# A two-layer decoder trunk on one core: a planner that simulates the timeline in place of the default planner

## The chip, the cores and the metric

The kernel runs on one core of a Trainium2 chip, as one launch. A core has five engines that each work through a queue of their own: TensorE (PE in the profile, with its weight loads shown apart as PEld), VectorE (DVE), ScalarE (ACT), GpSimd (POOL) and SyncE (SP), which here only issues DMA transfers. They wait for each other by semaphores. The metric is the device time of the launch in microseconds; lower is better.

## The reference

The input is one sequence of 512 tokens with 1024 features, in float32. Layer 0 runs multi-head latent attention (MLA, 8 heads) and differential attention (4 heads, each with two score matrices) side by side behind one input projection, layer 1 dilated attention (three groups of 4 heads) and stick-breaking attention (4 heads). Each mixer is followed by a gated ConvFFN of width 2816, and both are wrapped in RMSNorms with a residual.

```python
for i in range(DEPTH):                      # DEPTH = 2
    h = rms_norm(x, pre_g)
    h = even_mixer(h, ...) if i % 2 == 0 else odd_mixer(h, ...)
    x = x + rms_norm(h, post_g)
    h = conv_ffn(rms_norm(x, ffn_pre_g[i]), ffn_w_up[i], ffn_conv_w[i], ffn_conv_b[i], ffn_w_down[i])
    x = x + rms_norm(h, ffn_post_g[i])

# the differential heads of even_mixer, for one block of 128 queries
def probs(qb, kf):
    s = jnp.einsum('bhqd,bhkd->bhqk', qb, kf).astype(jnp.float32) * scale + bias   # ALiBi
    return jax.nn.softmax(jnp.where(causal, s, -jnp.inf), axis=-1)
p = probs(a1, k1) - lam * probs(a2, k2)
o = jnp.einsum('bhqk,bhkd->bhqd', p.astype(v.dtype), v)
o_diff = rms_norm(o_diff, subln_g) * (1.0 - lam_init)

# the stick-breaking heads of odd_mixer
log_beta = jax.nn.log_sigmoid(z)
log_keep = jnp.where(strict, jax.nn.log_sigmoid(-z), 0.0)
after = lax.cumsum(log_keep, axis=3, reverse=True) - log_keep
a = jnp.where(strict, jnp.exp(log_beta + after), 0.0)

def conv_ffn(h, w_up, conv_w, conv_b, w_down):
    gate, up = jnp.split(causal_dwconv(h @ w_up, conv_w, conv_b), 2, axis=-1)
    return (jax.nn.silu(gate) * up) @ w_down
```

## The kernel before

**Products.** Every float32 product with a weight is done as three products of a shorter type. An operand is split into a high part, cast on ACT, and a remainder, subtracted on DVE; `mm3` (L263 to L265) then issues high × high, high × low and low × high into one PSUM bank. Weights come in units of 128 x 1024: SP loads the raw unit, ACT casts it (`wh`, L72) and DVE subtracts (`wl`, L73). The class `Weights` holds several units loaded ahead and splits them ahead of their use. Activations are split by the helper `split` (L171, L172).

**Stages.** The program runs `even`, `ffn(0)`, `odd`, `ffn(1)` one after the other. The 512 tokens are four tiles of 128 rows; the results of the projections are held by feature or by token as the next stage needs them. PSUM banks are handed out under five tags: `a` (3 banks), `s` (2), `t`, `o` and `n` (1 each). A new use of a bank waits for the last reader of the old one.

**The attention stages.** `skewed` (L270 and following) runs a list of units in a software pipeline that is written out by hand: in one step it issues the scores of unit n, the transposes of unit n−1, the value product of unit n−2 and so on, and after every so many steps it takes one of a list of *fillers*, pieces of projection work that are independent of the units.

- In the even mixer, MLA comes first: 32 units of head and query tile (`score` with the reduction L593 and the exponential L597, `turn`, `value` L750). Its fillers are the four `diff_v` pieces (`av`, value projection of the differential heads, L755 to L769), which in program order stand at the end.
- Then come the differential heads: 16 units, four query tiles for each of four heads. `score` issues two score products (L827, one bank each) under `tc.high_priority()`, two reductions with the ALiBi table (L593), two exponentials (L597), and the combination of the two (L838 to L841). `turn` transposes it (L604) and copies it out of PSUM (L607 on ACT, L609 on DVE), `value` multiplies by the values (L852), scales (L854) and squares for the mean (L856 on ACT); POOL computes the reciprocal root (`rr`, L178 and L181) and `norm` applies it (L863). `finish` transposes a head's four tiles (`tpo`, L870) and splits them (`odh`, `odl`).
- The fillers of the differential heads, one every second step, are six groups of query and key projections (`aqk`, `diff_qk`, L622 to L631, 24 matmuls each) and four pieces of the output projection (`ao`, `project`, L880 to L895), whose MLA half needs only the MLA results `omh`, `oml`.
- The tables of the differential heads come by DMA from ACT's queue: `subg` (L780), `lamb` (L782) and `alibi` (L786). `lamb` leads to the scalar `neglam` (L790 to L796). They lie in a pool whose space comes free with the MLA stage.
- In the odd mixer the stick-breaking heads go through `sb_scores` (L1025 and following, Exp at L1044), `sb_softplus` (Ln at L1049) and `sb_weights` (split `sh`, `sl`, then the suffix sums as products `cp`, L1064, and Exp at L1068). Exp and Ln need different tables of ACT, and a change of table is an ACT_TABLE_LOAD of 1.28 us. The dilated heads follow as two pipelines with `apt` (L968 to L980) and `apv` projections as fillers.

**What sets the order.** The program text gives a first order and all dependencies. Each engine's queue is then laid out by the planner of the tile framework: it goes through the program with a model of the engines, and among the instructions that could come next it chooses by a priority that follows program order and by when the model says that operands and buffers are there. Three kinds of place are not free: `tc.manual_schedule` keeps the written order of the named engines (the ends of the even mixer, L905 to L930, of the last FFN, about L508 to L565, and of the odd mixer, about L1262 to L1290), `tc.high_priority()` pulls the differential score products forward, and `keep_in_program_order` and `add_manual_dep` bind single instructions. All else is what the change calls the free parts. The planner is set where the kernel opens its context, `tile.TileContext(nc)` at L1395.

## Time and profile before

| | us |
|---|---|
| median of three runs | 1167.63 |
| lowest and highest | 1166.95, 1168.72 |
| span of the profiled execution, first to last instruction | 1165.2 |
| median less that span, what lies around it | 2.4 |
| mean granted TensorE clock | 0.998 |

The page of the profile gives each engine's busy time, the span in 40 slices, the chain that ended last and the costliest groups of instructions. A group's row has the line, engine, operation, output and inputs with their shapes, the count, busy time, mean duration in ns, and the idle time of the engine ahead of it with what ended that idle time. In the timeline a row has its start, its duration, and in brackets the idle time before it and the releaser. Matmuls are pipelined: a row of 390 ns may be followed by the next 0.23 us later. PE's ends are modelled, so a busy PE isn't necessarily a PE at its peak. Where the stages lie in the span: input projections to 63.9 us, MLA attention to 119.9, differential attention to 207.7, then the end of the even mixer, the first FFN to some 600, the odd mixer to some 820, and the second FFN.

### The profile page before, as it was taken

How to read it: one execution, taken by the hardware profiler on the slowest of the kernel's cores; microseconds unless marked ns; L12 is line 12 of the kernel's file. 1: busy time of each engine (PE TensorE's matmuls, PEld its weight loads, DVE VectorE, ACT ScalarE, POOL GpSimd, SP SyncE). 2: the span in 40 equal slices, each digit the busy share in tenths (PEclk: the TensorE clock that was granted, in tenths of full speed). 3: DMA queues.
4: the chain of work that ended last, by engine and by line, in shares of the span. 5: the costliest groups of instructions: out<-in, count | busy, mean ns of one | idle time of the engine just before them, and what ended most of it. 6: DMA issues, size and time to landing. Idle time of an engine off the chain costs nothing.

```text
span 1165.2 us, 15209 instructions
## 1 busy us (share of the span) xinstructions
PE 1145.4 (98%) x5668; PEld 939.9 (81%) x5668; DVE 812.3 (70%) x1431; ACT 556.9 (48%) x940; POOL 57.5 (5%) x137
## 2 busy tenths in 40 slices
PE   8999999999999999999999999999999999999997
PEld 8876667898888888888878877898988888888886
DVE  6677676457766767899873465666676766779896
ACT  5565555245444444456553454544444444445562
POOL 2100012110000000000020000002000000000002
PEclk9999999999999999999999999999999999999999
DMA  8320521033332332354735212322232323324461
GB/s 283 115 64 1 169 73 38 37 130 127 95 104 91 104 95 82 109 159 155 246 108 159 73 55 91 91 74 83 95 116 91 102 98 91 106 84 136 138 214 72
DMA packets 39049, 126.81 MB, mean 109 GB/s; under 512 B 4672, under 2 KB 6336, under 8 KB 38848
## 3 DMA queue, kind: packets, MB, share of 16 engines
q1 hardware_dynamic: 37056, 122.11, 32.8%
q10 hardware_dynamic: 1920, 3.74, 1.0%
q8 instruction: 44, 0.72, 0.3%
q14 instruction: 29, 0.24, 0.1%
HBM read 117.95 MB, written 6.29 MB: 107 GB/s over the span
## 4 chain that ended last, share of the span: by engine, by line
PE 45%; issue 2%; DVE 1%; POOL 1%; ACT 1%; POOLq 0%; DVEq 0%; ACTq 0%
PE u L265 7%; PE u L264 7%; PE u L263 7%; PE acc L263 3%; PE acc L265 3%; PE acc L264 3%; PE apt L263 3%; PE apt L264 3%; PE apt L265 2%; PE cp L1064 1%; PE apv L263 1%; PE apv L265 1%; PE apv L264 1%; PE o L1148 1%; PE o L1225 1%
## 5 line engine op out<-in xcount | busy, mean ns | idle before, releaser
L73 DVE TENSOR_TENSOR wl<-wraw,wh 128x1024 fp32r<-128x1024 f32 (+1 forms) x202 | 244.5, 1218 | 182.2 <-ACT wh L72 178.0
L72 ACT CAST wh<-wraw 128x1024 fp32r<-128x1024 f32 (+1 forms) x202 | 209.4, 1046 | 281.2 <-PE u L264 179.6
L264 PE MATMUL u<-xl,wh 128*128 128x512 f32 (+1 forms) x768 | 285.3, 372 | 0.1
L265 PE MATMUL u<-xh,wl 128*128 128x512 f32 (+1 forms) x768 | 285.2, 372 | 0.0
L263 PE MATMUL u<-xh,wh 128*128 128x512 f32 (+1 forms) x768 | 285.0, 372 | 0.1
L264 PEld LDWEIGHTS u<-xl,wh 128*128 128x128 f32 x768 | 144.7, 188 | 25.3 <-DVE xl L172 0.3
L263 PEld LDWEIGHTS u<-xh,wh 128*128 128x128 f32 x768 | 144.5, 188 | 25.4 <-ACT xh L171 0.6
L265 PEld LDWEIGHTS u<-xh,wl 128*128 128x128 f32 x768 | 144.7, 188 | 24.9
L264 PE MATMUL acc<-wl,gh 128*128 128x512 f32 (+1 forms) x250 | 96.9, 387 | 0.0
L265 PE MATMUL acc<-wh,gl 128*128 128x512 f32 (+1 forms) x250 | 96.9, 387 | 0.0
L263 PE MATMUL acc<-wh,gh 128*128 128x512 f32 (+1 forms) x250 | 96.8, 388 | 0.0
L417 ACT ACTIVATE y<-y 128x512 f32<-128x512 f32 x44 | 27.7, 632 | 85.1 <-DVE y L415 85.1
L412 ACT ACTIVATE y<-u,cw 128x512 f32<-128x512 f32 x88 | 67.4, 773 | 1.8 <-PE u L265 1.8
L415 DVE SCALAR_TENSOR_TENSOR y<-u,cw,y 128x510 f32<-128x510 f32 x88 | 65.6, 748 | 2.5
L413 DVE SCALAR_TENSOR_TENSOR y<-u,cw,y 128x511 f32<-128x511 f32 x88 | 65.1, 744 | 0.9 <-ACT y L412 0.9
L178 POOL TENSOR_TENSOR rv<-ms,epst 128x1 f32<-128x1 f32 x39 | 11.0, 285 | 924.1 <-ACT junk L230 843.9
L263 PEld LDWEIGHTS acc<-wh,gh 128*128 128x128 f32 x250 | 46.9, 188 | 10.0 <-issue 0.6
L265 PEld LDWEIGHTS acc<-wh,gl 128*128 128x128 f32 x250 | 46.9, 188 | 9.7
L264 PEld LDWEIGHTS acc<-wl,gh 128*128 128x128 f32 x250 | 46.9, 188 | 9.6
L263 PE MATMUL apt<-xh,wh 128*128 128x512 f32 x128 | 50.6, 395 | 0.0
L264 PE MATMUL apt<-xl,wh 128*128 128x512 f32 x128 | 50.0, 391 | 0.0
L265 PE MATMUL apt<-xh,wl 128*128 128x512 f32 x128 | 49.9, 390 | 0.0
(305 smaller groups left out, 1911.3 us busy)
## 6 DMA issues: line engine op xcount, KB each, us to landing
wraw<-in_ffn_w_up SPq DMA_DIRECT2D x88, 512.0 KB, 3.6
wraw<-in_ffn_w_down SPq DMA_DIRECT2D x44, 512.0 KB, 3.7
wraw<-in_od_w_dqk SPq DMA_DIRECT2D x12, 512.0 KB, 3.6
wraw<-in_ffn_w_down SPq DMA_DIRECT2D x22, 256.0 KB, 2.6
wraw<-in_ev_w_dqk SPq DMA_DIRECT2D x8, 512.0 KB, 4.0
wraw<-in_ev_w_out SPq DMA_DIRECT2D x8, 512.0 KB, 3.7
spill<-X SPq DMA_DIRECT2D x8, 512.0 KB, 2.6
X<-spill SPq DMA_DIRECT2D x8, 512.0 KB, 6.6
```

Source lines behind the costliest of these rows:

```text
L72: self.nc.scalar.copy(h[:, :w], raw[:, :w])
L73: self.nc.vector.tensor_tensor(l[:, :w], raw[:, :w], h[:, :w].bitcast(F32), ALU.subtract)
L263: PE.matmul(o, lh, rh, start=first, stop=False, skip_group_check=more)
L264: PE.matmul(o, lh, rl, start=False, stop=False, skip_group_check=more)
L265: PE.matmul(o, ll, rh, start=False, stop=last, skip_group_check=more)
L412: ACT.activation(y[:, z], u, AF.Identity, bias=c[:, 3:4], scale=c[:, 2:3])
L413: DVE.scalar_tensor_tensor(y[:, z, 1:], u[:, :S - 1], c[:, 1:2], y[:, z, 1:], ALU.mult, ALU.add)
L415: DVE.scalar_tensor_tensor(y[:, z, 2:], u[:, :S - 2], c[:, 0:1], y[:, z, 2:], ALU.mult, ALU.add)
L417: ACT.activation(y[:, 0], y[:, 0], AF.Silu)
L1064: PE.matmul(zp[:, c + (j2 - j) * P:c + n], tri[:, 0 if j2 == j else 1], part[:, off[j2]:off[j2 + 1]], start=(j2 == j and part is sh), stop ...
L1148: PE.matmul(o12[hp][:, y, r], pt[:, y, rr, g], cv12[:, r, c:c + 64], start=(g == 0), stop=(g == 1))
L1225: PE.matmul(o[:, h], pt[:, h, b * P:(b + 1) * P], cv[:, j0 + b, h * 64:(h + 1) * 64], start=(b == 0), stop=(b == nb - 1))
```

## The change

One argument is added where the context is opened. The planner that lays out the free parts then keeps a simulation of the whole timeline, with the engines and their semaphores, and chooses the next instruction by what that simulation says, in place of the default model. No instruction's operation, shape, operands or buffer is written otherwise, and the sections that are kept in written order stay.

```diff
--- before.py
+++ after.py
@@ -1392,7 +1392,7 @@
     A = {n: nc.dram_tensor(f"in_{n}", v.shape, mybir.dt.from_np(v.dtype), kind="ExternalInput").ap()
          for n, v in arrays.items()}
     out = nc.dram_tensor("out_0_dram", (S, D), F32, kind="ExternalOutput").ap()
-    with tile.TileContext(nc) as tc:
+    with tile.TileContext(nc, schedule_with_timeline_sim=True) as tc:
         trunk(tc, A, out)
     r = run_bass_kernel_spmd(nc, [{f"in_{n}": v for n, v in arrays.items()}], core_ids=[0])
     return r.results[0]["out_0_dram"].reshape(1, S, D)
```

In the built program the same compute instructions stand on each engine as before, in another order; two ACT_TABLE_LOADs come in addition (ten in place of eight), and some semaphore waits differ.

## The prediction, made before the changed kernel ran

> **What bounds the kernel now.** I read the page's engine shares and clock first, then the chain that ended last, then windows of single stages.
>
> ```profile
> span 1165.2 us, 15209 instructions
> PE 1145.4 (98%) x5668; PEld 939.9 (81%) x5668; DVE 812.3 (70%) x1431; ACT 556.9 (48%) x940; POOL 57.5 (5%) x137
> PEclk9999999999999999999999999999999999999999
> PE 45%; issue 2%; DVE 1%; POOL 1%; ACT 1%; POOLq 0%; DVEq 0%; ACTq 0%
> ```
>
> TensorE (PE) is busy for 1145.4 of 1165.2 us at the full clock, and nothing else has more than 1% of the chain apart from issue. So at most 19.8 us of PE idling can be won by any order of the same instructions, and an order loses as soon as it puts PE behind something. Averages don't say where that may happen; these windows do (us from the span's start, then length, then busy time of PE, weight loads, VectorE (DVE), ScalarE (ACT), GpSimd (POOL), granted clock, DMA share, GB/s):
>
> ```profile
> 8.70:12.90 4.20, 1.55 (x8) 1.00 (x8) 2.71 (x4) 3.08 (x6) 0.74 (x2) 1.00 1.03 420
> 12.90:16.30 3.40, 3.40 (x11) 3.21 (x11) 3.39 (x5) 2.22 (x4) 0.94 (x2) 0.50 0.56 169
> 63.90:119.90 56.00, 55.90 (x270) 35.63 (x268) 40.89 (x159) 31.08 (x96) 0.00 (x0) 1.00 0.11 34
> 119.90:207.70 87.80, 83.84 (x429) 61.40 (x430) 60.82 (x196) 45.72 (x126) 13.88 (x32) 1.00 0.30 93
> 130.00:140.00 10.00, 7.89 (x37) 5.09 (x35) 7.50 (x16) 6.68 (x12) 0.00 (x0) 1.00 0.74 246
> 187.30:199.50 12.20, 12.20 (x74) 9.09 (x72) 9.90 (x43) 7.52 (x27) 3.48 (x8) 1.00 0.11 44
> 580.00:600.00 20.00, 18.41 (x88) 14.57 (x87) 15.82 (x21) 10.87 (x22) 7.92 (x17) 1.00 0.23 80
> 650.00:660.00 10.00, 9.05 (x50) 6.87 (x50) 7.11 (x12) 5.00 (x6) 0.00 (x0) 1.00 0.37 107
> 850.00:900.00 50.00, 50.00 (x223) 41.38 (x222) 32.94 (x44) 20.40 (x25) 0.00 (x0) 1.00 0.35 105
> ```
>
> 63.9 to 119.9 is the MLA attention, 119.9 to 207.7 the differential attention. In both PE is full: 99.8% and 95%. In the second, PE carries 83.84 us and DVE 60.82: long chains on DVE, ACT and POOL are hidden under projection matmuls that were put between the units. That cover is what an order can give away.
>
> **The change part by part.** The instructions are the same but for two more activation-table loads. I compare the built order of the two programs, engine by engine, and place each difference by the amount of PE work ahead of it.
>
> *Even mixer.* This is the one large move.
>
> ```profile
> L263 PE MATMUL aqk<-xh,wh 128*128 128x512 f32 x48 | 19.7, 411 | 0.0
> L265 PE MATMUL av<-wh,xl 128*128 128x512 f32 x14 | 5.6, 398 | 0.0
> L263 PE MATMUL ao<-wh,omh 128*128 128x512 f32 x12 | 5.2, 436 | 0.0
> ```
>
> Before, 232 projection matmuls stand on PE between the last MLA value matmul and the last transpose of the differential heads (the rows show one of the three products each for `aqk`, `av` and most of `ao`); after the change 57 do. The other 175 (most of the products for `av`, all six groups for `aqk`) stand inside the MLA stretch, together with nine weight splits on DVE and ACT and four copies of results. Their PE work doesn't vanish: row 850 to 900 has 223 matmuls in 50 us, 0.224 each, so 175 × 0.224 = 39.2 us more in the MLA stretch, where PE is already full and DVE (40.89 of 56) has room for nine splits. What the differential stretch then needs I take from its DVE side:
>
> ```profile
> L73 DVE TENSOR_TENSOR wl<-wraw,wh 128x1024 fp32r<-128x1024 f32 x12 | 14.6, 1221 | 3.3 <-ACT wh L72 3.3
> L863 DVE SCALAR_TENSOR_TENSOR otok<-otok,rr,subg 128x128 f32<-128x128 f32 x16 | 5.6, 349 | 10.6 <-POOL rr L181 10.5
> L631 DVE COPY dqk<-aqk 128x512 f32<-128x512 f32 x3 | 2.1, 689 | 2.4 <-PE aqk L265 2.4
> L767 DVE COPY dv<-av 128x512 f32<-128x512 f32 x1 | 0.7, 686 | 0.0
> ```
>
> DVE keeps 60.82 − 9 × 1.22 − 2.1 − 0.7 = 47.0 us, PE keeps 83.84 − 39.2 = 44.6. The stretch changes from PE-bound to DVE-bound, with chains on top.
>
> Its start first. The score reduction L593 needs the ALiBi table, 1 MB, whose load stands on ACT's queue behind the cast `omh` of the last MLA value. The new order leaves it there, since its space comes free with the MLA pool:
>
> ```profile
> 119.92 0.59 ACT L171 CAST omh<-o 128x512 fp32r<-128x512 f32 x1 [2.18 <-PE o L750]
> 120.78 0.45 ACTq L786 DMA_DIRECT2D alibi<-in_alibi  x1
> 125.33 0.23 DVE L790 CUSTOM_DVE_ANT_0 lj<-lamb 128x64 f32<-128x64 f32 x1 [1.78 <-DMA lamb<-in_ev_lam]
> 128.38 0.69 DVE L593 CUSTOM_DVE_ANT_0 s<-sps,alibi 128x512 f32<-128x512 f32 x1
> alibi<-in_alibi ACTq DMA_DIRECT2D x1, 1024.0 KB, 7.6
> ```
>
> So 120.78 + 7.6 = 128.38: no differential score can start for 8.5 us after 119.9. Before, `av` and `aqk` products filled that time. Now 20 output-projection matmuls (about 4.5 us) are left, and the weights for them stand on DVE behind `lamb`'s arrival (125.33).
>
> Then the pace. The last head of before, with no `aqk` group left beside it, is nearest to the new state:
>
> ```profile
> 187.34 0.68 DVE L593 CUSTOM_DVE_ANT_0 s<-sps,alibi 128x512 f32<-128x512 f32 x1
> 190.97 0.55 DVE L593 CUSTOM_DVE_ANT_0 s<-sps,alibi 128x384 f32<-128x384 f32 x1
> 193.70 0.42 DVE L593 CUSTOM_DVE_ANT_0 s<-sps,alibi 128x256 f32<-128x256 f32 x1
> 196.45 0.27 DVE L593 CUSTOM_DVE_ANT_0 s<-sps,alibi 128x128 f32<-128x128 f32 x1
> ...
> 199.35 0.35 DVE L840 SCALAR_TENSOR_TENSOR s<-s,den 128x128 f32<-128x128 f32 x1
> 204.57 0.35 DVE L854 TENSOR_SCALAR otok<-o,den 128x128 f32<-128x128 f32 x1 [0.58 <-PE o L852]
> 207.15 0.60 PE L870 MATMUL tpo<-ident,otok 128*128 128x128 f32 x4
> ```
>
> Three unit steps take 9.11 us, 3.04 each, so 12.15 a head and 48.6 for four. After the last score the last unit still drains: 204.57 to 207.75 is 3.2 us from its scaling to its transposes, and about 1.8 (an estimate) goes to the transpose, copy and value matmul in front, 5.0 together. The four splits left in the stretch are three more than in that head's window; two of them I put on the path (2.4), and 3 us for one group of 24 output products (24 × 0.224 = 5.4) in which DVE has little to do. Sum: 8.5 + 48.6 + 5.0 + 2.4 + 3 = 67.5 us. With the moved 39.2 this is 106.7 where 87.8 stood: **+18.9**. Bounds: if DVE runs without gaps, four heads cost 47.0 less the four splits, 42.1, and with 8.5 and 5.0 the stretch is 55.6: +7. If the waits on POOL that L863 shows (10.6 us) all fall on the pace, 78.1: +29.5. I take the measured pace.
>
> The Trainium skill ("Perfetto Trace Analysis", section "Optimization Strategy") says that regimes bound by different engines may gain from being interleaved. Here the new order separates two such regimes; before's row of 83.84 and 60.82 us in 87.8 agrees with the rule, and no run here shows the opposite order yet.
>
> *First FFN to odd mixer.*
>
> ```profile
> 586.37 1.32 PE L211 MATMUL tp<-ident,t 128*128 128x128 f32 x8 [1.37 <-DVE t L201]
> 658.65 2.44 ACT L1044 ACTIVATE sp<-sp 128x1280 f32<-128x1280 f32 x2 [3.62 <-DVE sp L1043]
> 664.12 1.28 ACT L1049 ACT_TABLE_LOAD   x1
> ```
>
> PE is idle for 1.6 us of 580 to 600 (20.00 − 18.41). The new order puts the last transposes behind all products of the bank, with two casts and two squares in ACT's queue ahead of the cast that they feed. About 4 us of waiting (an estimate, two 1 us ACT instructions over what stands) in place of 2: **+2**, from 0 if other products cover it to +3.
>
> *Odd mixer.* Stick-breaking's Exp and Ln were done in pairs; now they alternate: two more table loads of 1.28 us on the chain from `sp` to the first suffix product L1064. One Exp is 1.22 us, so the first ends at 659.9; a load, one Ln, a maximum and the cast `sh` (each over 1 us) follow, with a weight cast among them: about 666, while PE would have reached that product at 662.2. That is 3.8 of waiting against the 0.95 in row 650 to 660: +2.8. Near the end of the mixer DVE's work catches up with PE's (10.4 in 10 us, counted from before's durations in the new order): +1.5, an estimate. Together about **+4**, from +1 to +8.
>
> *Head.*
>
> ```profile
> 9.13 1.06 ACT L188 ACTIVATE junk<-X 128x1024 bf16<-128x1024 f32 x1 [0.46 <-DMA X<-in_x]
> 10.80 0.46 PE L263 MATMUL ac<-wh,xh 128*128 128x416 f32 x1 [2.08 <-ACT xh L171]
> wraw<-in_ev_w_dqk SPq DMA_DIRECT2D x8, 512.0 KB, 4.0
> ```
>
> ACT no longer has one square of 1.05 us ahead of the first cast of `xh`: **−0.5**, 0 to −1. Five small loads pass one weight load on SP's queue; that weight is needed only after 24 us of PE work, so this costs nothing, and some 4 us (one weight load's landing) if that cover were gone. Both FFNs and the hand-ordered ends stand as before: 0, since their work keeps its place relative to PE.
>
> Sum: 18.9 + 2 + 4 − 0.5 = 24.4, of which I keep **+23.5**, as one of the waits in hand-over and odd mixer may hide under the other's products. The profiled execution's span is 1165.2; the median of the runs is 1167.6, so 2.4 lie around the span, unchanged. 1165.2 + 2.4 + 23.5 = **1191**.
>
> **The rivals.** (a) *The clock falls.* In row 8.7 to 12.9 PE is busy for 1.55 of 4.2 us, and the next 3.4 us run at 0.50. If the thinner differential stretch (44.6 of 67.5) does the same in half of its some 17 stretches of 3.4 us past the table's wait, PE loses 1.7 us in each, and about two thirds of that (its busy share) lengthens the stretch: +10, 1201. Against it: 130 to 140 has PE at 7.89 of 10 and the clock at 1.00, and the idle pieces should be about 1 us each. The Trainium skill ("TensorE: Matmul & The Clock Gate", "What's actually happening") has the clock halved after one idle window of about 3.4 us and restored after a busy one; by it only the table's wait would cost, about 1.7 us. (b) *The planner hides the chains*: DVE runs gapless in the differential stretch, +7, with +2 elsewhere: 1177. For it: only 9.90 of 12.20 us were DVE's in the last head, where PE was full. Against: L863 waits on POOL in every unit. (c) *Faster.* The new order closes some of PE's 19.8 us of idling (4.2 in the differential stretch, 1.6 and 0.95 above, 2.6 in the first window) and the differential stretch is bounded by PE. That needs DVE, ACT and POOL to keep to 44.6 us plus a table landing in advance; it decides from the point where the 8.5 us are filled. Then −5: 1162. Against: DVE's 47.0 is already over 44.6 and the table's load stays behind `omh`. (d) *Nothing moves*: out, since the built order differs; but both effects could cancel near 1168.
>
> **How the numbers follow.** Forecast 0.65, its own range 1183 to 1200 (pace and odd mixer); (a) 0.10; (b) 0.17; (c) 0.05; (d) 0.03. The range reaches down to (b)'s 1177 less a little, 1175, and up to +29.5 in the even mixer with +3 and +8 behind it, 1208. About 0.2% (2.3 us) is what a measurement of this kernel tells from no change: faster 0.05, same 0.03, slower 0.92.
>
> **What would show it.** In the changed profile: the MLA stretch some 39 us longer with PE still full; then L593 on the table beginning 8 to 9 us after the last `omh`, PE idle for some 4 us of it; the differential stretch near 67 us with PE at about two thirds and DVE at 70%, DVE waiting for `rr` and for the exponentials; ten table loads, two in the odd mixer, and PE waiting at L1064. It is wrong if the even mixer's end moves by less than 7 us, if the clock drops there for long, or if the FFN stages change by over 1 us.

## The result, and the profile after

The changed kernel takes 1201.13 us (median of four runs, 1200.49 to 1203.24) against 1167.43 us before (1166.95 to 1168.72): a ratio of 1.0291, interval 1.0277 to 1.0306, or 33.7 us more. The forecast was 1191, the range 1175 to 1208. The time is just outside the 1183 to 1200 that were given for the forecast's own mechanism, and it is the 1201 that rival (a), the falling clock, had named; the part on the prediction comes back to both.

The page of the changed kernel, in the lines that were shown of before:

```profile
span 1199.0 us, 15219 instructions
...
PE 1162.5 (97%) x5668; PEld 950.7 (79%) x5668; DVE 811.5 (68%) x1431; ACT 560.8 (47%) x942; POOL 56.4 (5%) x137
...
PEclk9999989899999999999989999999999999999999
...
PE 44%; DVE 2%; issue 1%; ACT 1%; POOL 0%; DMA 0%; POOLq 0%; DVEq 0%; ACTq 0%
```

DVE does the same work as before (811.5 against 812.3). PE is busy for 17.1 us longer with the same matmuls (5668 records in both pages), and idle for 36.5 instead of 19.8 us. So half of the loss is PE waiting, and half is PE working more slowly; the row of granted clocks has three eights that before didn't have.

Where it was lost follows from the starts and ends of the same instructions in both profiles (us from the span's start; the last column is what was added since the row above):

| | before | after | later by | added |
|---|---|---|---|---|
| last cast `omh`, the end of MLA | 119.92 | 160.75 | 40.8 | (fillers moved in) |
| cast `odh` behind the last differential transposes | 207.78 | 227.53 | 19.8 | 19.8 in the even mixer |
| first product of the first FFN | 242.1 | 262.7 | 20.6 | 0.8 |
| its first down product | 484.9 | 505.2 | 20.3 | −0.3 |
| first `apv` product of the odd mixer | 640.7 | 665.0 | 24.3 | 4.0 in the hand-over |
| last `apv` product of the odd mixer | 776.4 | 808.2 | 31.8 | 7.5 in the odd mixer |
| last down product of the second FFN | 1157.6 | 1189.6 | 32.0 | 0.2 |
| last instruction | 1165.2 | 1199.0 | 33.8 | 1.8 in the last rows |

The windows of the changed kernel that answer to those of before, with the same columns; the first runs from the input projections to the end of MLA, the second is the differential stretch, the third its first 8.2 us, then two places in it, then the hand-over to the odd mixer:

```profile
30.00:160.75 130.75, 130.20 (x605) 97.21 (x603) 76.88 (x207) 60.65 (x143) 2.78 (x7) 1.00 0.25 75
160.75:227.50 66.75, 49.30 (x253) 32.85 (x253) 46.78 (x183) 34.03 (x113) 13.17 (x32) 0.91 0.16 51
160.70:168.90 8.20, 2.50 (x8) 1.69 (x8) 3.75 (x10) 2.78 (x4) 0.00 (x0) 0.72 0.51 157
190.00:195.00 5.00, 3.88 (x11) 3.02 (x11) 3.17 (x11) 0.93 (x4) 0.37 (x1) 0.66 0.30 105
225.00:230.00 5.00, 2.92 (x8) 2.17 (x9) 1.19 (x3) 0.58 (x1) 0.74 (x2) 0.57 0.00 0
600.00:620.00 20.00, 15.99 (x70) 12.88 (x69) 17.20 (x22) 10.17 (x21) 7.63 (x13) 0.87 0.37 132
```

PE stays full (130.20 of 130.75) up to the end of MLA, so the moved fillers cost their own time there. The stretch behind it fell from 87.8 to 66.75 us, with PE busy for 49.30 and the clock at 0.91. The timeline of the changed kernel shows how the stretch begins, on three engines, and how it ends (start, duration, engine, line, operation, and in brackets the idle time and what ended it); the last line is the table's load, with its size and the time to its landing:

```profile
160.75 0.58 ACT L171 CAST omh<-o 128x512 fp32r<-128x512 f32 x1 [2.18 <-PE o L750]
161.60 0.45 ACTq L786 DMA_DIRECT2D alibi<-in_alibi  x1
163.27 1.27 PE L263 MATMUL ao<-wh,omh 128*128 128x512 f32 x4 [2.56 <-ACT wh L72]
166.00 0.23 DVE L790 CUSTOM_DVE_ANT_0 lj<-lamb 128x64 f32<-128x64 f32 x1 [1.45 <-DMA lamb<-in_ev_lam]
166.41 2.36 DVE L73 TENSOR_TENSOR wl<-wraw,wh 128x1024 fp32r<-128x1024 f32 x2
167.69 0.79 PE L264 MATMUL ao<-wl,omh 128*128 128x512 f32 x1 [3.14 <-DVE wl L73]
168.94 0.68 DVE L593 CUSTOM_DVE_ANT_0 s<-sps,alibi 128x512 f32<-128x512 f32 x1
...
219.92 0.35 DVE L840 SCALAR_TENSOR_TENSOR s<-s,den 128x128 f32<-128x128 f32 x1
226.41 1.08 PE L870 MATMUL tpo<-ident,otok 128*128 128x128 f32 x4 [2.31 <-DVE otok L863]
...
alibi<-in_alibi ACTq DMA_DIRECT2D x1, 1024.0 KB, 6.8
```

The table is issued behind `omh`, the first reduction on it starts 8.2 us after `omh` started, and the output products that could have run meanwhile wait for a weight remainder that stands on DVE behind `lamb`: as forecast, with one shift. The table landed at 168.4 (161.60 + 6.8), and two weight remainders held DVE until 168.8, so that the last 0.4 us before the reduction are theirs. At the end PE waits 2.31 us for the last normalised tile.

### The profile page after: what moved, and what is told of

Read it like the earlier page. It is cut to its first block, busy times and chain, and to the rows that moved or that the text cites. A ratio compares the mean times of both kernels' runs of the same rounds, so it can differ in the third digit from the quotient of the medians.

```text
span 1199.0 us, 15219 instructions
## 1 busy us (share of the span) xinstructions
PE 1162.5 (97%) x5668; PEld 950.7 (79%) x5668; DVE 811.5 (68%) x1431; ACT 560.8 (47%) x942; POOL 56.4 (5%) x137
## 5 line engine op out<-in xcount | busy, mean ns | idle before, releaser
L263 PE MATMUL acc<-wh,gh 128*128 128x512 f32 (+1 forms) x250 | 87.2, 388 | 1.0 <-DVE uu L480 1.0
L178 POOL TENSOR_TENSOR rv<-ms,epst 128x1 f32<-128x1 f32 x39 | 10.2, 265 | 939.8 <-ACT junk L230 858.6
L597 ACT ACTIVATE s<-s,st 128x128 f32<-128x128 f32 (+3 forms) x64 | 35.8, 559 | 39.7 <-DVE st L593 38.3
```

The lines of the kernel that those rows point to most:

```text
L263: PE.matmul(o, lh, rh, start=first, stop=False, skip_group_check=more)
L597: ACT.activation(s[:, :n], s[:, :n], AF.Exp, bias=st[:, 0:1], scale=-1.0, accum_out=st[:, 1:2])
```

## The experiments

Two tools were used. In the first, one stage or one engine is held to an order: the instructions of the engine in the stage are chained by edges that bind the issue order only and add no wait. The order is that of the other kernel, one list of instruction numbers for each engine (`ORDERS`; "all engines" means PE, DVE, ACT and POOL, while the loads on SP stay free), so that the rest of the program remains as its planner lays it out:

```diff
+    edge = mybir.DependencyInfo(mybir.DependencyClass.NoSync, mybir.DependencyReason.DATA)
+    for text in ORDERS:
...
+        for first, then in zip(names, names[1:]):
+            tc.add_manual_dep(traced[then], first, edge, reason="order")
...
         trunk(tc, A, out)
+        pin(tc, nc)
```

In the second, the new planner stays free and the source is edited.

| run | planner | what is held or edited | time, us | ratio to before, interval |
|---|---|---|---|---|
| e_even | default | even mixer, all engines, new order | 1190.9 | 1.0209, 1.0194 to 1.0223 |
| e_turn | default | hand-over FFN to odd mixer, new order | 1169.6 | 1.0022, 1.0013 to 1.0030 |
| e_odd | default | odd attention, new order | 1174.2 | 1.0059, 1.0046 to 1.0072 |
| e_head | default | head, new order | 1166.5 | 0.9996, 0.9988 to 1.0005 |
| n_fill | new | all fillers kept behind MLA | 1198.0 | 1.0267, 1.0252 to 1.0281 |
| n_fill23 | new | `aqk` of heads 2 and 3 kept in place | 1198.9 | 1.0274, 1.0257 to 1.0291 |
| n_table | new | table in four pieces, issued first | 1194.4 | 1.0243, 1.0219 to 1.0267 |
| n_keep | new | PE kept busy before the last transposes | 1198.2 | 1.0268, 1.0253 to 1.0283 |
| n_av | new | last two `av` and all `aqk` behind MLA | 1191.0 | 1.0201, 1.0186 to 1.0216 |
| o_odd_pe | default | odd attention, PE alone, new order | 1174.4 | 1.0059, 1.0047 to 1.0071 |
| o_odd_act | default | odd attention, ACT alone, new order | 1181.2 | 1.0115, 1.0099 to 1.0131 |
| n_even_pe | new | even mixer, PE alone, order of before | 1184.4 | 1.0139, 1.0120 to 1.0158 |

The kernel before, run beside them, had medians of 1166.9 to 1167.3 us.

### What does each stage cost by itself?

> The default planner, with only the even mixer (from the MLA projections to the output projection) held to the order that the new planner gives it. In the changed kernel's profile the first product of the first FFN starts 20.6 us later than before (262.7 against 242.1), with 1.8 us already won in the head. Theory: the price belongs to this stage alone, so the time is 1167.4 + 20.6 + 1.8 = 1190, from 1187 to 1192, and the granted clock falls in three places as in the changed kernel. Rival: a part of the loss comes from what stands around it (the head's gain, the loads that the new order issues earlier), then the time is under 1185. Second rival, that the whole loss of 33.7 us starts here and only shows later: 1197 or more.

> The default planner, with only the end of the first FFN and the first projections of the odd mixer held to the new order. In the changed kernel's profile PE waits 1.25 and 2.76 us there for a cast and a subtraction, and matmuls run at half clock for about 5 us after it; before has 1.6 and 0.9 us of idling in the same place. Theory: +4 us, 1171.5 (1170 to 1173). Rival: the waits are only exchanged for waits that the default order has in the same place, under +1.5 us.

> The default planner, with only the attention of the odd mixer held to the new order, so with its two more table loads and with PE going 39 instead of 32 times from small products to projections. Theory: +7 us, 1174.5 (1172.5 to 1176.5), as no idle time of PE stands in the changed profile there, it comes as slower progress of PE. Rival: the lost time is the waiting at the hand-over that moved on, then under +2 us.

> The default planner, with only the head (input normalisation and first projection) held to the new order. In the changed profile the first projection matmul starts at 9.20 instead of 10.80 and the last at 33.4 instead of 35.2. Theory: the 1.8 us stay to the end, as PE is full behind it: 1165.6 (1165.0 to 1166.4), faster than before. Rival: they are lost at the next wait for a weight or a table, 1167.4.

Against 1167.1 us beside them, the even mixer costs 23.8 us, the hand-over 2.5, the odd attention 7.1 (1174.2, in the expected 1172.5 to 1176.5), and the head −0.6, which is within what a measurement tells from nothing. The sum is 32.8 of 33.7 us. So the rival of a price that only moves on is out, and the rest of about 1 us can stand for the last rows of the program, where the table of starts has 1.8; which order is at fault there wasn't tried. The even mixer's price is at the upper end of what was expected (1190.9 in 1187 to 1192); the clock fell at both ends of its differential stretch, but not in the middle as in the changed kernel. The hand-over came out just under the 1170 to 1173 expected, and its largest wait is that of the changed profile. Its row in the list of PE's waits (line waiting, releaser, us in all, times, longest):

```profile
PE tp L211 <- DVE xl L172: 2.8, 1, 2.8
```

That the prices add up to within 1 us is partly luck. In e_even the first FFN product starts 21.2 us later than in before (263.3), but the last down product 23.7 (1181.3): some 2.5 us of that price came behind the stage, where the order is that of before. In the changed kernel the stage itself costs 22.4 (20.6, and the 1.8 that the head had won), and the hand-over 4.0 instead of 2.5. The granted clock goes with both differences; in the hand-over PE also idled for 0.5 us longer. The same 20 us of the hand-over, in the changed kernel and in e_turn, and then a window of the odd mixer in e_even, whose counterpart in before (650 to 660, also with 9.05 us of PE) had 1.00:

```profile
605.00:625.00 20.00, 15.99 (x68) 12.77 (x68) 17.05 (x23) 10.92 (x21) 8.37 (x15) 0.83 0.30 105
585.00:605.00 20.00, 16.49 (x76) 13.28 (x75) 16.01 (x21) 11.47 (x23) 8.72 (x17) 0.91 0.31 105
672.40:682.40 10.00, 9.05 (x46) 6.73 (x45) 7.12 (x13) 4.95 (x6) 0.00 (x0) 0.87 0.33 107
```

The head starts its products earlier, but little or nothing of it shows in the time, which lies above the 1165.0 to 1166.4 expected. In its profile 1.9 us are still won at the first scores of the odd mixer (650.37 against 652.31), and 1.6 of them are lost in that mixer, to the clock, and not at a wait for a weight or a table, as the rival had it. The same instructions, in the same order and behind the same wait, first in e_head, then in before:

```profile
654.01 0.92 PE L1033 MATMUL zp<-sq,sk 64*128 64x256 f32 x4 [0.82 <-DVE z L1037]
...
655.92 0.63 PE L263 MATMUL apt<-xh,wh 128*128 128x512 f32 x1
```

```profile
655.95 0.92 PE L1033 MATMUL zp<-sq,sk 64*128 64x256 f32 x4 [0.82 <-DVE z L1037]
...
657.59 0.40 PE L263 MATMUL apt<-xh,wh 128*128 128x512 f32 x1
```

### The even mixer: is it the cover?

The edit of n_fill; n_fill23 holds only `h > 1`, without `diff_v`:

```diff
-            PE.matmul(o, lh, rh, start=first, stop=False, skip_group_check=more)
+            m = PE.matmul(o, lh, rh, start=first, stop=False, skip_group_check=more)
+            if hold:
+                tc.keep_in_program_order(m)
...
-                                xh[:, k], xl[:, k], k == 0, k == KD - 1)
+                                xh[:, k], xl[:, k], k == 0, k == KD - 1, hold=k == 0 and h > 0)
...
-                            mm3(a, xh[:, k, t], xl[:, k, t], wh[:, c], wl[:, c], k == 0, k == KD - 1)
+                            mm3(a, xh[:, k, t], xl[:, k, t], wh[:, c], wl[:, c], k == 0, k == KD - 1, hold=k == 0)
```

> The new planner, but the first product of every filler of the differential heads (four groups of av, six of aqk, 240 matmuls) is kept behind what was traced before it on PE, so that the fillers can't leave the differential stretch for the MLA stretch; all else stays free. Theory: the loss of the even mixer (23.8 us when this stage alone has the new order) comes from the place of the fillers. With them back the stretch has its cover again: 1201.1 - 20 = 1181 (1177 to 1186), clock 1.00 in the stretch. Rival: the new order of the units' own work on DVE, ACT and POOL is what costs, then the fillers only swap places and the time stays over 1193.

> The same for the four aqk groups of heads 2 and 3 alone (96 matmuls, 21.5 us of PE work at 0.224 each). Theory: the stretch of 66.8 us had 17.5 us of idle PE and some of it at half clock; the 96 matmuls fill most of what lies in the middle, but not the wait for the table at its start. 1201.1 - 11 = 1190 (1186 to 1194). Rival: a linear price by matmul (20 us for 175) gives the same 1190, so this run tells whether half the cover suffices (then 1184 or less) or only all of it does (then 1197 or more).

Both expectations fell: 3 and 2 us came back, not 20 and 11. By n_fill23 half of the cover is not enough, and by n_fill all of it isn't either. The window over the MLA stretch of n_fill says why:

```profile
63.90:119.30 55.40, 49.18 (x209) 25.28 (x210) 40.06 (x157) 28.74 (x95) 0.00 (x0) 0.97 0.10 34
```

MLA ends at 119.3 us, as in before (119.92), though it has lost the 56 `av` products that before ran in it: PE is busy for 49.18 of 55.40 us where before had 55.90 of 56.00. With all fillers behind MLA, MLA has no cover. What had been a question of the differential stretch is a question of two stretches that share one stock of fillers, and of where in each they lie. In n_fill23 the wait for the table at the start is still uncovered.

> The new planner; the last two groups of av (48 matmuls) are kept behind the last MLA value product. As aqk takes the same PSUM banks later, its six groups stay behind them too: 192 filler matmuls in the differential stretch (before has 184), 96 projections in the MLA stretch (before 56), where 48 and none stood when all four groups were held. Theory: that earlier run lost in the MLA stretch what it won behind it, as MLA had no cover left (it took 56 us with 56 matmuls less); here both stretches are covered and the 48 av products fill the 8.2 us in which the table lands. 1201.1 - 18 = 1183 (1179 to 1188). Rival: the order of the units' own work costs as much as the missing cover: 1193 or more.

```diff
+                                    final = PE.matmul(o[y * 64:(y + 1) * 64, j * P:], mv[:, j, h * 64:(h + 1) * 64],
...
+                            ends.append(final.ins.name)
...
+            if after:
+                tc.add_manual_dep(m.ins, after, ORDERED, reason="order")
...
-                            mm3(a, xh[:, k, t], xl[:, k, t], wh[:, c], wl[:, c], k == 0, k == KD - 1)
+                            mm3(a, xh[:, k, t], xl[:, k, t], wh[:, c], wl[:, c], k == 0, k == KD - 1, after=ends[-1] if k == 0 and i > 1 else None)
```

Here `ORDERED` is an edge of issue order only, as above. 10.2 us came back, more than from any other edit of the source, but neither the 18 of the theory nor the 8 or less of its rival. Two windows of n_av, one in MLA and one at the end of the differential stretch, show the places that are left:

```profile
80.00:110.00 30.00, 27.10 (x124) 13.84 (x122) 23.27 (x97) 17.04 (x58) 0.00 (x0) 1.00 0.00 1
200.00:217.00 17.00, 12.19 (x74) 8.33 (x72) 13.18 (x52) 9.39 (x35) 6.80 (x15) 0.93 0.01 1
```

2.9 us of idle PE lie in the middle of MLA and 4.8 at the end of the heads, where before has output products.

> The new planner, with PE alone held to the order of before in the even mixer; DVE, ACT and POOL follow the new planner (154 of DVE's places in this stage differ from before). With 192 fillers brought back, 10 of the even mixer's 23.8 us came back; in that profile the MLA stretch ran with PE at 9.0 of 10 from 80 to 110 us and the differential stretch ended with PE at 8.05 and 6.47 of 10, where before has output products. Theory: what is left is also a matter of which products stand beside which unit, and PE's order alone carries the whole price: 1201.1 - 22 = 1179 (1176.5 to 1182). Rival: the new order of the units' own steps on DVE, ACT and POOL carries the rest: 1188 or more.

With PE alone held to the order of before, 16.7 of the 23.8 us return (16 to 20 by the ends of the interval); the expectation was 22, its rival at most 13. The first FFN product starts at 246.4 us, 4.3 later than in before. One wait in n_even_pe accounts for most of that:

```profile
141.50 1.86 PE L852 MATMUL o<-dv,pt 128*128 128x128 f32 x7 [4.17 <-ACT pt L607]
...
140.00:145.00 5.00, 3.50 (x12) 3.19 (x13) 3.07 (x10) 2.94 (x8) 0.45 (x2) 0.50 0.75 240
```

PE waits 4.17 us for a copy on ACT, which stands on ACT behind weight casts that wait for their loads, and the clock drops during the wait. The 16.7 us lie between the theory and its rival: PE's order carries some 70% of the stage's price (16.7 of 23.8). Much of what is left lies in one place where ACT's order doesn't fit PE's; this is read from the rows and wasn't tried alone, and the planner laid ACT out anew around the held PE.

### The wait for the table, and the clock

> The new planner; the ALiBi table is loaded in four pieces by head, issued ahead of subg and lamb. In the changed profile the table is issued at 161.6 and the first reduction starts at 168.94, and the weight remainders for the output products stand behind lamb at 166.4. Theory: the wait for the table is on the path now; the first piece lands some 3 to 4 us earlier, but lamb comes later and the first combination needs it: 1201.1 - 2.5 = 1198.6 (1197 to 1200). Rival: PE's order behind it (20 output products) or the chains set the stretch's length: no gain, 1201.

```diff
+                alibi = sc.tile([P, 4, S], F32, tag="alibi", name="alibi")
+                for h in range(4):
+                    nc.scalar.dma_start(alibi[:, h], A["alibi"][:, h])
                 nc.scalar.dma_start(subg[:], A["ev_subln_g"][0:1, :].partition_broadcast(P))
...
-                alibi = sc.tile([P, 4, S], F32, tag="alibi", name="alibi")
-                nc.scalar.dma_start(alibi[:], A["alibi"])
```

> The new planner; ahead of the last transposes of the differential heads 21 transposes of the last head's finished tiles are repeated, 2.3 us of PE work in the 2.3 us that PE sits idle there (224.1 to 226.4), so that PE doesn't pause. In the changed profile the transposes and 10 products behind that pause run at half clock (0.43 us apart instead of 0.23). Theory: the clock costs 2.5 us there, 1201.1 - 2.4 = 1198.7 (1197.5 to 1200), and the granted clock is 1.00 in that place. Rival: work behind it waits for DVE anyway, or the clock falls all the same: 1201 or more.

```diff
                         tp = bank("t", "tpo", NT, P)
+                        for i in ORDER[:-1] * (7 if h == 3 else 0):
+                            PE.transpose(tp[:, i], otoks[h][:, i], ident[:])
```

The first rows are n_table's timeline, with `omh` at 161.8 us there; then n_keep's timeline and its window over the same 5 us as after's row at 225:

```profile
164.76 0.69 DVE L593 CUSTOM_DVE_ANT_0 s<-sps,alibi 128x512 f32<-128x512 f32 x1 [1.66 <-DMA alibi<-in_alibi]
...
166.13 1.65 PE L828 MATMUL sps<-dqk 64*128 64x384 f32 x4 [4.37 <-DVE st L593]
```

```profile
225.44 2.51 PE L870 MATMUL tpo<-ident,otok 128*128 128x128 f32 x21
227.82 0.66 PE L872 MATMUL tpo<-ident,otok 128*128 128x128 f32 x4
```

```profile
225.00:230.00 5.00, 4.21 (x30) 3.36 (x31) 1.81 (x5) 0.99 (x3) 0.95 (x3) 1.00 0.00 0
```

In n_table the first reduction starts 3.0 us after `omh` instead of 8.2, and the kernel gains 6.8 us by the medians; its runs spread (1192.0 to 1199.6), and by the ends of its interval the gain is 3 to 8.5 us. The wait for the table is on the path, the rival (no gain) is out, and the gain is larger than the 2.5 us expected; its size is open between these, as the profiled execution is the slowest of the five. In n_keep the 21 transposes stand where PE had paused, the clock is 1.00 where it was 0.57, and four transposes take 0.66 instead of 1.08 us. The time falls by 3.0 us by the medians, against 2.4 expected; its interval and that of the changed kernel overlap slightly (1.0283 and 1.0277), so the mechanism is shown by the rows and the size only roughly. The granted clocks of all four executions agree: 0.990 to 0.993, against 0.987 or 0.988 in the changed kernel.

### The odd mixer: PE's order or the table loads?

> The default planner, with PE alone held to the new order in the odd mixer's attention; ACT and DVE are free and ACT has eight table loads. With all engines held this stage costs 7.1 us. Theory: PE's own order costs, as it goes more often from small products (L1033, L1074, L1148, L1178: 8, 4, 9, 8 runs of them in place of 2, 2, 3, 4) to projections: +5 us, 1172 (1170.5 to 1174). Rival, the step of the prediction: the two table loads on the chain to L1064 cost, then this order without them is within 1.5 us of before.

> The default planner, with ACT alone held to the new order in the odd mixer's attention, so with ten table loads; PE and DVE are free. Theory: at most the two loads show, 1.28 us each, and PE has other products meanwhile: +0 to +2.6, 1168.5. Rival, the step of the prediction: the loads hold up the suffix products: +4 to +7, 1171 to 1174.

PE's order alone costs 7.1 us, the price of the whole stage, while ACT keeps the loads of before in it. The ACT groups of the odd mixer, first in the changed kernel, then in o_odd_pe:

```profile
L1049 ACT ACT_TABLE_LOAD x3 | 3.8, 1283 | 0.1
L1044 ACT ACT_TABLE_LOAD x2 | 2.6, 1283 | 0.0
```

```profile
L1049 ACT ACT_TABLE_LOAD x2 | 2.6, 1283 | 0.0
...
L1044 ACT ACT_TABLE_LOAD x1 | 1.3, 1283 | 0.0
```

So the two extra loads are not needed to explain the loss. o_odd_act says less than it was made for: it cost 13.9 us, above both expectations, but the default planner, bound on ACT, reordered PE as well, so that it isn't a price of ACT's order.

What in PE's order costs is read from the timeline of the scores L1178, in before:

```profile
761.02 1.14 PE L1178 MATMUL z<-ck,cq 64*128 64x256 f32 x8
762.09 0.39 PE L263 MATMUL apv<-wh,xh 128*128 128x256 f32 x1
```

and in the changed kernel:

```profile
789.99 0.70 PE L1178 MATMUL z<-ck,cq 64*128 64x256 f32 x2
790.62 0.44 PE L1131 MATMUL t<-ident,s 128*128 128x128 f32 x2
790.98 0.70 PE L1178 MATMUL z<-ck,cq 64*128 64x256 f32 x2
...
793.88 1.13 PE L1178 MATMUL z<-ck,cq 64*128 64x256 f32 x4
```

Each of these products uses 64 of PE's 128 rows; the two heads of a pair lie in opposite halves. The profile counts each product twice (32 in this group, where the program issues 16), so the row of before holds four products. Before orders them first half, second half, first, second, and the four take 1.14 us, 0.28 each. The new order has two of the first half, each alone among transposes and value products (0.70 us for one), and later the two of the second half behind each other (1.13 us for two, 0.57 each); the list of o_odd_pe has them as numbers 6608, 6610, 6609 and 6611 of the program. No wait stands there, and the mean duration of one record hardly changes (376 and 379 ns); what is lost is that neighbours in different halves run at the same time. Groups of the same lines in the odd mixer, before and then after:

```profile
L1074 PE MATMUL osb<-z,sv 128*64 128x512 f32 (+3 forms) x32 | 4.7, 439 | 0.0
...
L1178 PE MATMUL z<-ck,cq 64*128 64x256 f32 (+1 forms) x32 | 4.1, 376 | 0.0
```

```profile
L1178 PE MATMUL z<-ck,cq 64*128 64x256 f32 (+1 forms) x32 | 7.7, 379 | 0.0
L1074 PE MATMUL osb<-z,sv 128*64 128x512 f32 (+3 forms) x32 | 6.9, 442 | 0.0
```

3.6 us more for L1178 and 2.2 for L1074 (its pairs lie in two halves of PE's columns), with the same count and nearly the same mean: 5.8 us of busy time, where the stage costs 7.1. That is not yet a price: in o_odd_pe L1033, also on half the rows, took 1.7 us more (8.6 for 6.9), L1148 0.7 more and L1064 1.1 less, and 1.3 us of idle time ahead of L1033 went. The Trainium skill ("TensorEngine Tiling (Array Packing)", section "Key Properties") says that different tiles of the array run matmuls in parallel; the rows above agree. That restoring the alternation alone returns the time was not tried, so the cause is PE's order as a whole by experiment, and the lost alternation by reading. o_odd_act, with PE in a third order, fits it: there L1109, also in pairs of halves, took 7.1 us for 4.6, and L1074 6.9.

## Why the prediction was right, point by point

- **Direction, main place and mechanism: right.** The fillers left the differential stretch, and the cover went with them. The stage's price was forecast as 18.9 us and measured as 23.8 with this stage alone (22.4 by the starts in the changed kernel).
- **The moved work.** 39.2 us were forecast; the end of MLA moved by 40.8 although the head had gained 1 to 2 us, so it was some 42, or 0.24 us for each of 175 matmuls instead of 0.224.
- **The start of the stretch.** 8.5 us forecast, 8.2 measured, the last 0.4 of it on DVE and not on the table; the wait for `lamb` in front of the weight remainder is there, and n_table shows that the wait is on the path.
- **The length of the stretch.** 67.5 forecast, 66.75 measured, but its parts were off on both sides. From the first reduction to the last unit's combination it took 51.0 us (168.94 to 219.92), where 48.6 + 2.4 + 3 = 54.0 were forecast; the drain behind it took 7.6 (to 227.53) instead of 5.0; the same two points lie 8.4 apart in before (199.35 to 207.78). That the sum fits is luck, the more so as the 66.75 us hold lost clock that no term had.
- **The clock, rival (a): it came, beside the forecast's mechanism and not in its place.** A clock of 0.91 over 66.75 us is 6.0 us of full-speed work lost; the rival had priced 10. Over the whole span the mean clock of 0.988, for 0.998 before, stands for some 12 us of lost full-speed work, a part of it in idle time. The rival's 1201 is the time that came, though not by its mechanism alone: the moved work (2.8 us) and the odd mixer (3.1) were short in the forecast as well. I had held the clock at 1.00 because a window of before with PE at 7.89 of 10 kept it. A long drop of the clock there is also one of the signs named for a wrong forecast. The step failed: one window was taken for a rule. Two of the three falls lie at the ends of the stretch, where PE has single waits of 2.3 to 3.1 us; the third (0.66 in 190 to 195) stands behind waits of 0.74, 0.64 and 1.12 us, the idle pieces of about 1 us that I had held harmless. Behind the stretch the output products at half clock add to it.
- **The hand-over.** +2 forecast, 2.5 measured with this part alone and 4.0 by the starts in the changed kernel, by the wait that was named (a remainder queued behind other work) and a fall of the clock with it (0.83 in 605 to 625), which wasn't.
- **The odd mixer: mis-sized, and for the wrong reason.** +4 was forecast, +2.8 of it from two table loads ahead of L1064. 7.1 were measured, without the loads, from PE's order, and the changed kernel's list of PE's waits has none at L1064. The step took PE's work as a sum of durations that doesn't depend on the neighbours.
- **The head.** −0.5 forecast, −0.6 measured, not distinguishable from none. Both FFNs: 0 forecast, −0.3 and 0.2 in the table of starts. The tail: 0 forecast, 1.8 in the table. The chain to the end goes through POOL's L540, which starts 0.4 us ahead of the last down product in before (1157.44 against 1157.87) and 1.3 behind it in the changed kernel (1191.14 against 1189.87); why the row norm runs later there was not tried.
- **The sum.** 33.7 instead of 23.5: 4.9 too little for the even mixer, 3.1 for the odd, 0.5 for the hand-over, and the 0.9 that was struck off for an overlap of which the runs show nothing. About 1 us is open. By the starts in the changed kernel the misses lie a little otherwise: 3.5 in the even mixer, 2.0 in the hand-over, 3.5 in the odd mixer and 1.8 in the tail, less 1.3 that the head won over its forecast.
- **Rival (b)**, gapless DVE, is out: DVE was busy for 46.78 us, close to the 47.0 forecast, of 66.75. **Rival (c)**, faster: PE's idling grew from 19.8 to 36.5 us. The point it was to be decided by, the 8.5 us of the table, is where it failed. **Rival (d)**, nothing moves, is out by the time.

## What to carry to other kernels

A filler that is ready early is worth most where nothing else can run: before a planner is let loose, list the waits that only fillers cover (a table behind a pool's end, a drain, a chain through several engines) and hold fillers there, but leave enough for the stretch that they are taken from. A busy share of PE near 100% is no proof that PE does its work at the least cost: compare the busy time of the same group, at the same count and mean, between two orders. When a planner breaks several stages, hold one stage of one kernel to the order of the other; prices that add up tell where to look, but beside a price of 1 or 2 us look at the granted clock: a fall of it, present in one execution and not in another, cost e_head 1.6 us.

## What the runs showed of the hardware

- The clock fell after shorter pauses than I had expected. In the changed kernel PE waits for 2.31 us from 224.1 on, and the clock was at half already within that wait, after some 1.6 us of it (1.00 over 224.1 to 225.6, 0.50 over 225.7 to 228.1). With 2.5 us of transposes in that place it was 1.00. The Trainium skill ("TensorE: Matmul & The Clock Gate", section "Why this matters for your kernels") warns of pauses over some 3 us; here PE paused for 2.31 us and again for 0.68, so the measurement decides: less was enough.
- Whether a pause costs differs from one execution to the next. Behind the same wait of 0.82 us, in the same order, products ran at half clock in e_head (0.63 us a row; 0.87 over 672.4 to 682.4 in e_even) and at full clock in before (0.40 us, 1.00 over 650 to 660).
- Score products on half of PE's rows cost 0.28 us each when the halves alternate and 0.57 when they don't, with nothing in the list of waits and hardly a change in the mean duration of a record.
